# Low parts of normed operands, of the sums T1 to T4 and of the first gate and up weights on VectorE alone

## The chip, the cores and the metric

The kernel runs on one core of a Trainium2 chip. The core has a TensorE for matmuls (PE; its weight loads are PEld), VectorE (DVE), ScalarE (ACT), GpSimd (POOL) and a queue that issues DMAs (SP). The metric is the time on the device in microseconds, from one launch; each version is run several times and the median counts.

## The reference

The kernel computes two layers of an encoder for 1024 positions of width 1024, in float32. Cut to what matters here:

```
h = rms_norm(x, mix_norm_g[l])                 # x * rsqrt(mean(x*x) + eps) * g
proj = h @ w_in[l]                             # then three mixers: retention, RWKV-7, differential attention
x = x + mixed @ w_out[l]
h = rms_norm(x, ffn_norm_g[l])
hidden = silu(h @ w_gate[l]) * (h @ w_up[l])   # width 2816
x = x + hidden @ w_down[l]
...                                            # after both layers a last rms_norm
```

## The kernel before

All activations lie transposed: 8 row blocks of 128 features by two halves of 512 positions, so a tile is 128x512. The matmuls must be more exact than TensorE's fast format, so each operand is split: ScalarE copies it to the fast format (the high part, names ending in h: hh, sh, whh) and another engine subtracts the copy from the original (the low part: hl, sl, wll). `split` (lines 177 to 186) does both; its subtraction runs on VectorE unless `eng` says GpSimd. A product is then three matmuls, high by high, low by high and high by low (`dense`). In the names of the profile, h tiles are normed operands and T1, s tiles are T2 to T4, w tiles are weights; wr is a raw weight block from memory, ws a sum of weights.

The feed-forward part (`phase_c`) comes after the mixers. It first multiplies by w_out (`out_blocks`, PSUM tiles aps), norms both halves of the result (`norm_sq`, `norm_rs`, `norm_out`: squares on ScalarE, their sum on VectorE, a matmul with ones, nps, then logarithm and exponential on ScalarE, nrs, and a product on VectorE, line 262), and then computes gate and up in 11 pairs of column blocks (q = 0 to 10, 256 columns each). Each pair of each matrix is one Winograd-Strassen step over 2x2 blocks: seven block products instead of eight. The seven use the blocks B11, B21 and B22 of the normed input and its sums T1 to T4 (`ops_sums`: T1 = B12 - B11, T2 = B22 - T1, T3 = T2 - B11, T4 = B21 - T2, each for four row blocks), and of the weights A11, A12, A22 and four sums S1 to S4 (`set_first`, `set_rest`). The products are the tiles sp; there are seven PSUM banks for them. The input's low parts are made once per layer, at the start; the weights' low parts for each q. The wh and wl tiles have 8 buffers each, so a ninth weight part waits for the products that use the first.

Before the change, of the input's low parts GpSimd makes every second one of B11, B21, B22, T2 and T4 and all of T1 and T3, and it makes all of the weights'. The same alternation stands in `norm_split`, which norms the input of the mixers at each layer's start (tiles ntmp, products dps with w_in).

A scheduler sets the order of each engine's instructions from the program's order, its own estimates and priorities (`high_priority` around the norms). Each engine runs its queue strictly in order. During the mixers' input projection only one raw weight block fits (`wraw` is 1 with 4 row blocks), so the DMA of the next block is sent only when the high and the low part of the one before are made.

Of the kernel before, what the change touches and what calls it, by code (L numbers as in the profile page):

```python
# [177 lines left out]
class Net:  # L178
# [8 lines left out]
    def tt(self, out, a, b, op, eng=None):  # L187
        (eng or self.nc.vector).tensor_tensor(out=out, in0=a, in1=b, op=op)  # L188
# [87 lines left out]
    def norm_split(self, x, g, pool):  # L276

        h = [[], []]

        def emit(half, k, t):  # L280
            h[half].append(self.split(self.H, t, ("h", "h"), eng=self.nc.gpsimd if k % 2 else None))

        self.norm(x, g, pool, emit, (1, 0))
        return h
# [1004 lines left out]

    def op(self, ops, name, t, eng=None):
        p, tag = (self.S, "s") if name in ("T2", "T3", "T4") else (self.H, "h")
        ops[name].append(self.split(p, t, (tag, tag), eng=eng))

    def ops_sums(self, ops, bs, names=("T1", "T2", "T3", "T4")):

        g = self.nc.gpsimd
        for n in names:
            for i, (b11, b12, b21, b22) in enumerate(bs):  # L1300
                e = g if i % 2 else None
                if n == "T1":
                    self.tt(b12, b12, b11, ALU.subtract)
                    self.op(ops, n, b12, g)
                elif n == "T2":
                    self.tt(b22, b22, b12, ALU.subtract)
                    self.op(ops, n, b22, e)
                elif n == "T3":
                    self.tt(b11, b22, b11, ALU.subtract)
                    self.op(ops, n, b11, g)  # L1310
                else:
                    self.tt(b21, b21, b22, ALU.subtract)
                    self.op(ops, n, b21, e)

    def set_load(self, src):

        raw = []
        for a in src:
            r = self.W.tile([128, 8, 128], F32, tag="wr", name="wr", bufs=self.wraw)
            self.nc.sync.dma_start(out=r, in_=a)  # L1320
            raw.append(r)
        a, b = raw
        return dict(A11=a[:, :4], A12=a[:, 4:], A21=b[:, :4], A22=b[:, 4:], w={})

    def set_split(self, st, src, *names):

        hi, lo = self.split(self.W, src, ("wh", "wl"), eng=self.nc.gpsimd)
        n = src.shape[1] // len(names)
        for i, name in enumerate(names):
            st["w"][name] = [(hi[:, i * n + k], lo[:, i * n + k]) for k in range(n)]  # L1330
# [42 lines left out]

    def ffn_set(self, l, name, q):
        w = self.ia[name]
        return self.set_load([w[l, 2 * q], w[l, 2 * q + 1]])

    def ffn_first(self, st, ops):
        a = self.ft("as")
# [30 lines left out]
    def phase_c(self, l):  # L1410
        nc = self.nc
        acts = [[], []]
        for half in range(2):
            for k in range(8):
                m = self.S.tile([128, 512], F32, tag="s", name="mixl")
                nc.sync.dma_start(out=m, in_=self.mixed[k][:, half * 512:half * 512 + 512])
                acts[half].append(self.split(self.H, m, ("h", "h")))
        x = self.load_x(self.xs)
        self.out_blocks(l, x, acts)

        xm = [self.dr.tile([128, T], F32, name=f"xm{l}_{k}") for k in range(8)]
        ops = {n: [] for n in ("B11", "B21", "B22", "T1", "T2", "T3", "T4")}
        g = self.par[l][:, P_FFNG:P_FFNG + 8]
        n = [dict(pool=(self.S, "s")) for _ in range(2)]
        gp = nc.gpsimd
        with self.tc.high_priority(offset=100000):
            for half in range(2):
                for k in range(8):
                    nc.sync.dma_start(out=xm[k][:, half * 512:half * 512 + 512], in_=x[half][k])
            self.norm_sq(n[0], x[0], range(8))  # L1430
            self.norm_sq(n[1], x[1], range(4))
            self.norm_rs(n[0])
            for k in range(8):
                self.op(ops, "B21" if k >= 4 else "B11", self.norm_out(n[0], g, k, x[0], x[0][k]),
                        gp if k % 2 else None)
            self.norm_sq(n[1], x[1], range(4, 8))
            self.norm_rs(n[1])
            for k in (4, 5, 6, 7, 0, 1, 2, 3):
                t = self.norm_out(n[1], g, k, x[1], x[1][k])
                if k >= 4:  # L1440
                    self.op(ops, "B22", t, gp if k % 2 else None)
            self.ops_sums(ops, [(x[0][i], x[1][i], x[0][i + 4], x[1][i + 4]) for i in range(4)])

        hid = [self.dr.tile([128, T], F32, name=f"hid{l}_{f}") for f in range(NF)]
        for q in range(NF // 2):
            sets = []
            for name in ("w_gate", "w_up"):
                st = self.ffn_set(l, name, q)
                self.set_first(st)
                if q == 0:  # L1450
                    self.ffn_first(st, ops)
                    self.set_rest(st)
                    sets.append(st)
                else:
                    self.ffn_part(st, ops, sets, hid, q)
            if q == 0:
                done = []
                for st in sets:
                    self.ffn_part(st, ops, done, hid, q)
        return self.down(l, hid, xm)  # L1460
# [175 lines left out]
```

## Time and profile before

| | us |
|---|---|
| median of three runs | 3579.34 (3575.51 to 3581.64) |
| the profiled execution | 3579.7 |
| its span, first to last instruction | 3577.9 |
| TensorE busy | 3222.8 (90%) |
| VectorE busy | 2004.6 (56%) |
| ScalarE busy | 1576.7 (44%) |
| GpSimd busy | 943.7 (26%) |

The shares are means over stages with different limits. The stages that the change touches are short: layer 0's start (20 to 60 us of the span), layer 1's start (about 1784 to 1822) and the two feed-forward starts (about 1073 to 1160 and 2841 to 2930). What counts there is read from the order of the instructions in time and from what each waited for.

### The profile page before, as it was taken

The numbers are of one execution on the slowest core, as the hardware profiler recorded it, in microseconds if no ns is written. First come the engines' busy times: TensorE is split into PE (matmuls) and PEld (weight loads), VectorE is DVE, ScalarE is ACT, GpSimd is POOL, SyncE is SP. The second block draws the span as 40 slices with busy tenths as digits, with TensorE's granted clock in tenths as the row PEclk, the third lists the DMA queues.
The fourth block names the chain that finished last, engine by engine and source line by source line (L and its number), as shares of the span: only waits on it lengthen the run. The fifth ranks groups of instructions, "written<-read, shape, count | busy, mean of one in ns | idle before, by whom it ended". The sixth has DMA issues, their size and how long they took to land. (4 is left out here: it accounts for less than half of the span.)

```text
span 3577.9 us, 69843 instructions
## 1 busy us (share of the span) xinstructions
PE 3222.8 (90%) x28380; PEld 2601.8 (73%) x28380; DVE 2004.6 (56%) x3749; ACT 1576.7 (44%) x3071; POOL 943.7 (26%) x800
## 2 busy tenths in 40 slices
PE   6999797898787999999989997978986989999997
PEld 4777586787565888888867775867774758888886
DVE  4698425766329555552338974167662485555523
ACT  4566443666424333342236664346654342333322
POOL 3222120000026544532132221200000364554220
PEclk9999798998888999999989998989988989999998
DMA  5444334432341222283053433244325212223821
GB/s 167 154 147 123 112 106 132 145 124 72 127 146 47 86 80 83 83 285 121 26 161 123 151 117 118 96 143 139 122 83 175 83 59 80 86 83 99 278 71 47
DMA packets 214057, 418.93 MB, mean 117 GB/s; under 512 B 23876, under 2 KB 58948, under 8 KB 213700
## 3 DMA queue, kind: packets, MB, share of 16 engines
q1 hardware_dynamic: 191000, 378.53, 32.2%
q10 hardware_dynamic: 12672, 23.07, 1.7%
q0 software_dynamic: 10064, 12.85, 1.6%
q8 instruction: 224, 3.67, 0.4%
q14 instruction: 97, 0.79, 0.1%
HBM read 313.67 MB, written 100.70 MB: 116 GB/s over the span
## 5 line engine op out<-in xcount | busy, mean ns | idle before, releaser
L188 POOL TENSOR_TENSOR wll<-wr,whh 128x512 fp32r<-128x512 f32 x416 | 558.4, 1345 | 1616.8 <-ACT whh L185 1610.9
L185 ACT ACTIVATE whh<-wr 128x512 fp32r<-128x512 f32 x416 | 261.1, 631 | 625.8 <-PE sp L194 166.0
L194 PE MATMUL dps<-hl,whh 128*128 128x512 f32 x960 | 383.7, 400 | 6.6 <-DVE hl L188 3.6
L194 PE MATMUL dps<-hh,whh 128*128 128x512 f32 x960 | 387.7, 404 | 1.1 <-DVE stl L377 1.0
L194 PE MATMUL dps<-hh,wll 128*128 128x512 f32 x960 | 383.1, 399 | 0.4 <-POOL wll L188 0.4
L194 PE MATMUL sp<-hh,whh 128*128 128x512 f32 x704 | 279.2, 397 | 9.2 <-ACT hh L185 8.6
L194 PE MATMUL sp<-hl,whh 128*128 128x512 f32 x704 | 281.8, 400 | 2.1 <-POOL hl L188 1.9
L194 PE MATMUL sp<-hh,wll 128*128 128x512 f32 x704 | 276.9, 393 | 1.3 <-POOL wll L188 1.3
L194 PE MATMUL dn<-hl,whh 128*128 128x512 f32 x704 | 274.9, 391 | 0.5 <-DVE hl L188 0.5
L194 PE MATMUL dn<-hh,whh 128*128 128x512 f32 x704 | 274.1, 389 | 1.3 <-ACT hh L185 1.3
L194 PE MATMUL dn<-hh,wll 128*128 128x512 f32 x704 | 273.9, 389 | 0.0
L188 POOL TENSOR_TENSOR wll<-ws,whh 128x512 fp32r<-128x512 f32 x132 | 194.1, 1470 | 177.2 <-ACT whh L185 177.2
L188 DVE TENSOR_TENSOR hl<-hidr,hh 128x512 fp32r<-128x512 f32 x144 | 138.2, 977 | 170.4 <-ACT hh L185 161.5
L194 PEld LDWEIGHTS dps<-hl,whh 128*128 128x128 f32 x960 | 183.6, 191 | 51.8 <-POOL hl L188 6.1
L194 PE MATMUL sp<-sl,whh 128*128 128x512 f32 x528 | 211.3, 400 | 8.8 <-POOL sl L188 6.1
L194 PEld LDWEIGHTS dps<-hh,whh 128*128 128x128 f32 x960 | 183.7, 191 | 45.9 <-issue 4.4
L194 PE MATMUL sp<-sh,whh 128*128 128x512 f32 x528 | 209.8, 397 | 3.1 <-ACT as L185 3.1
L194 PEld LDWEIGHTS dps<-hh,wll 128*128 128x128 f32 x960 | 183.2, 191 | 38.8 <-issue 2.4
L194 PE MATMUL sp<-sh,wll 128*128 128x512 f32 x528 | 211.0, 400 | 0.0
L185 ACT ACTIVATE whh<-ws 128x512 fp32r<-128x512 f32 x132 | 83.5, 632 | 242.7 <-PE sp L194 138.5
L185 ACT ACTIVATE pt<-pt,mx 128x1024 f32<-128x1024 f32 x128 | 147.0, 1149 | 59.6 <-DVE mx L1216 57.3
L194 PEld LDWEIGHTS sp<-hh,whh 128*128 128x128 f32 x704 | 133.9, 190 | 41.1 <-ACT hh L185 9.4
(275 smaller groups left out, 7297.6 us busy)
## 6 DMA issues: line engine op xcount, KB each, us to landing
hidr<-hid SPq DMA_DIRECT2D x144, 256.0 KB, 4.9
bias<-t SPq DMA_DIRECT2D x64, 512.0 KB, 3.8
wr<-in_w_in_dram SPq DMA_DIRECT2D x120, 256.0 KB, 2.9
wr<-in_w_gate_dram SPq DMA_DIRECT2D x44, 512.0 KB, 3.4
wr<-in_w_up_dram SPq DMA_DIRECT2D x44, 512.0 KB, 3.3
wr<-in_w_down_dram SPq DMA_DIRECT2D x44, 512.0 KB, 4.1
pr<-st SPq DMA_DIRECT2D x56, 256.0 KB, 2.3
lo<-lod SPq DMA_DIRECT2D x48, 256.0 KB, 3.2
```

The source lines that it names most:

```text
L185: self.nc.scalar.activation(out=out, in_=in_, func=func, **kw)
L188: (eng or self.nc.vector).tensor_tensor(out=out, in0=a, in1=b, op=op)
L194: self.nc.tensor.matmul(out, lhsT, rhs, start=start, stop=stop, **kw)
```

## The change

`norm_split`, `op` and `ops_sums` no longer name GpSimd, so every low part of the normed operands and of T1 to T4 is made by VectorE. A set of weights carries its engine: for the first pair (q = 0) of gate and up it is VectorE, for the others GpSimd as before.

```diff
@@ norm_split
-            h[half].append(self.split(self.H, t, ("h", "h"), eng=self.nc.gpsimd if k % 2 else None))
+            h[half].append(self.split(self.H, t, ("h", "h")))
@@ op, ops_sums
-    def op(self, ops, name, t, eng=None):
+    def op(self, ops, name, t):
         p, tag = (self.S, "s") if name in ("T2", "T3", "T4") else (self.H, "h")
-        ops[name].append(self.split(p, t, (tag, tag), eng=eng))
+        ops[name].append(self.split(p, t, (tag, tag)))
...
-                    self.op(ops, n, b12, g)
+                    self.op(ops, n, b12)
...
@@ set_load, set_split, ffn_set
-    def set_load(self, src):
+    def set_load(self, src, eng):
...
-        return dict(A11=a[:, :4], A12=a[:, 4:], A21=b[:, :4], A22=b[:, 4:], w={})
+        return dict(A11=a[:, :4], A12=a[:, 4:], A21=b[:, :4], A22=b[:, 4:], w={}, eng=eng)
...
-        hi, lo = self.split(self.W, src, ("wh", "wl"), eng=self.nc.gpsimd)
+        hi, lo = self.split(self.W, src, ("wh", "wl"), eng=st["eng"])
...
-        return self.set_load([w[l, 2 * q], w[l, 2 * q + 1]])
+        return self.set_load([w[l, 2 * q], w[l, 2 * q + 1]], self.nc.gpsimd if q else None)
@@ phase_c
-                self.op(ops, "B21" if k >= 4 else "B11", self.norm_out(n[0], g, k, x[0], x[0][k]),
-                        gp if k % 2 else None)
+                self.op(ops, "B21" if k >= 4 else "B11", self.norm_out(n[0], g, k, x[0], x[0][k]))
...
-                    self.op(ops, "B22", t, gp if k % 2 else None)
+                    self.op(ops, "B22", t)
```

VectorE's queue in layer 0's feed-forward start, from the first of T3 on (x_11643, x_11645, x_11647 and x_11649 become T3, x_11651 and the next T4), before:

```order
L188 TENSOR_TENSOR x_11643<-x_11667,x_11643 128x512
L188 TENSOR_TENSOR sl_12347<-x_11671,sh_12346 128x512
L188 TENSOR_TENSOR x_11645<-x_11669,x_11645 128x512
L188 TENSOR_TENSOR x_11647<-x_11671,x_11647 128x512
L188 TENSOR_TENSOR x_11649<-x_11673,x_11649 128x512
L188 TENSOR_TENSOR x_11651<-x_11651,x_11667 128x512
L188 TENSOR_TENSOR x_11653<-x_11653,x_11669 128x512
L188 TENSOR_TENSOR x_11655<-x_11655,x_11671 128x512
```

And after, the same subtractions:

```order
L188 TENSOR_TENSOR x_11643<-x_11667,x_11643 128x512
L188 TENSOR_TENSOR sl_12352<-x_11673,sh_12351 128x512
L188 TENSOR_TENSOR x_11645<-x_11669,x_11645 128x512
L188 TENSOR_TENSOR sl_12357<-x_11643,sh_12356 128x512
L188 TENSOR_TENSOR x_11647<-x_11671,x_11647 128x512
L188 TENSOR_TENSOR sl_12362<-x_11645,sh_12361 128x512
L188 TENSOR_TENSOR x_11649<-x_11673,x_11649 128x512
L188 TENSOR_TENSOR sl_12367<-x_11647,sh_12366 128x512
L188 TENSOR_TENSOR x_11651<-x_11651,x_11667 128x512
L188 TENSOR_TENSOR sl_12372<-x_11649,sh_12371 128x512
```

Between the subtractions, where one low part of T2 stood, there is now one for each operand.

VectorE's queue behind the last sums there (c11 and c12 are sums of products, ws_12527 becomes S4 of the up weights, sl_12387 and sl_12392 are low parts of T4), before:

```order
L188 TENSOR_TENSOR sl_12377<-x_11651,sh_12376 128x512
L188 TENSOR_TENSOR x_11657<-x_11657,x_11673 128x512
L188 TENSOR_TENSOR c11_12444<-sp_12445,as_12429 128x512
L188 TENSOR_TENSOR sl_12387<-x_11655,sh_12386 128x512
L188 TENSOR_TENSOR c11_12512<-sp_12513,as_12497 128x512
L188 TENSOR_TENSOR ws_12527<-wr_12485,ws_12528 128x512
L188 TENSOR_TENSOR c12_12553<-sp_12554,as_12429 128x512
```

And after:

```order
L188 TENSOR_TENSOR sl_12387<-x_11655,sh_12386 128x512
L188 TENSOR_TENSOR c11_12444<-sp_12445,as_12429 128x512
L188 TENSOR_TENSOR sl_12392<-x_11657,sh_12391 128x512
L188 TENSOR_TENSOR c11_12512<-sp_12513,as_12497 128x512
L188 TENSOR_TENSOR wll_12532<-ws_12528,whh_12531 128x512
L188 TENSOR_TENSOR wll_12537<-wr_12487,whh_12536 128x512
L188 TENSOR_TENSOR wll_12541<-ws_12527,whh_12540 128x512
L188 TENSOR_TENSOR c12_12553<-sp_12554,as_12429 128x512
L188 TENSOR_TENSOR ws_12527<-wr_12485,ws_12528 128x512
```

S4 of the up weights (ws_12527 <- wr_12485, ws_12528) now stands behind three low parts of up weights and a further sum of products.

ScalarE's queue in layer 1's start (whh_17766 is the high part of the second weight block, whh_17836 of the third; nrs_17640 is the second half's norm factor, first the logarithm, then the exponential), before:

```order
L185 ACTIVATE nsq_17632<-x_17485 128x512
L185 ACTIVATE nsq_17635<-x_17500 128x512
L185 ACTIVATE whh_17766<-wr_17764 128x512
L185 ACT_TABLE_LOAD
L185 ACTIVATE nrs_17640<-nps_17638,eps_116 128x512
L185 ACT_TABLE_LOAD
L185 ACTIVATE nrs_17640<-nrs_17640 128x512
L185 ACTIVATE whh_17836<-wr_17834 128x512
L185 ACTIVATE hh_17645<-ntmp_17643 128x512
```

And after:

```order
L185 ACTIVATE nsq_17632<-x_17485 128x512
L185 ACTIVATE nsq_17635<-x_17500 128x512
L185 ACTIVATE whh_17766<-wr_17764 128x512
L185 ACTIVATE whh_17836<-wr_17834 128x512
L185 ACT_TABLE_LOAD
L185 ACTIVATE nrs_17640<-nps_17638,eps_116 128x512
L185 ACT_TABLE_LOAD
L185 ACTIVATE nrs_17640<-nrs_17640 128x512
L185 ACTIVATE hh_17645<-ntmp_17643 128x512
```

The third block's high part moved from behind the exponential to ahead of the first table load.

## Rows read from the trace of the kernel before

**Rows 1.** Busy time by stretch, layer 0: length, PE, PEld, DVE, ACT, POOL, PEclk, DMA.

```profile
1072.94:1098.33 25.39, 17.12 (x76) 13.86 (x74) 23.39 (x24) 11.69 (x20) 18.47 (x11) 0.92 0.21 72
1103.93:1141.34 37.41, 26.10 (x83) 16.64 (x83) 37.41 (x32) 15.19 (x25) 28.24 (x18) 0.86 0.00 0
...
1160.00:1180.00 20.00, 20.00 (x89) 16.25 (x88) 14.74 (x22) 7.53 (x13) 13.31 (x10) 1.00 0.39 135
```

**Rows 2.** TensorE in order of time, layer 0's feed-forward start: start, duration, [idle before <-releaser].

```profile
1098.39 2.08 PE L194 MATMUL nps<-nsq,ones 128*128 128x512 f32 x2 [8.33 <-DVE nsq L188]
...
1139.06 0.80 PE L194 MATMUL sp<-sh,whh 128*128 128x512 f32 x1 [1.56 <-ACT as L185]
...
1140.08 0.63 PE L194 MATMUL sp<-sh,wll 128*128 128x512 f32 x1
1140.51 0.63 PE L194 MATMUL sp<-sh,whh 128*128 128x512 f32 x1
...
1143.80 0.50 PE L194 MATMUL sp<-hh,whh 128*128 128x512 f32 x1 [0.33 <-ACT whh L185]
...
1145.42 0.50 PE L194 MATMUL sp<-hh,wll 128*128 128x512 f32 x1 [0.66 <-POOL wll L188]
```

**Rows 3.** The chain that ended last, layer 1's feed-forward start: start, length, piece.

```profile
2896.81 8.43 DVE x L188 x5
...
2913.39 86.83 PE sp L194 x375
```

**Rows 4.** VectorE in order of time, layer 0's feed-forward start.

```profile
1072.94 2.08 DVE L262 SCALAR_TENSOR_TENSOR x<-x,par,nrs 128x512 f32<-128x512 f32 x3 [3.22 <-ACT nrs L185]
...
1097.64 0.69 DVE L188 TENSOR_TENSOR nsq<-nsq 128x512 f32<-128x512 f32 x1 [0.70 <-ACT nsq L185]
1103.93 4.16 DVE L262 SCALAR_TENSOR_TENSOR x<-x,par,nrs 128x512 f32<-128x512 f32 x3 [5.59 <-ACT nrs L185]
...
1126.94 1.28 DVE L188 TENSOR_TENSOR x<-x 128x512 f32<-128x512 f32 x2
1128.14 0.68 DVE L188 TENSOR_TENSOR sl<-x,sh 128x512 fp32r<-128x512 f32 x1
1128.75 9.11 DVE L188 TENSOR_TENSOR x<-x 128x512 f32<-128x512 f32 x6
...
1140.66 0.68 DVE L188 TENSOR_TENSOR sl<-x,sh 128x512 fp32r<-128x512 f32 x1
```

**Rows 5.** GpSimd in order of time, the same stretch.

```profile
1071.03 1.29 POOL L188 TENSOR_TENSOR wll<-wr,whh 128x512 fp32r<-128x512 f32 x1 [25.96 <-ACT whh L185]
...
1128.37 8.34 POOL L188 TENSOR_TENSOR sl<-x,sh 128x512 fp32r<-128x512 f32 x5 [1.90 <-ACT sh L185]
```

**Rows 6.** VectorE in order of time, layer 0's start.

```profile
20.37 2.08 DVE L262 SCALAR_TENSOR_TENSOR ntmp<-x,par,nrs 128x512 f32<-128x512 f32 x3 [4.22 <-ACT nrs L185]
...
33.49 5.55 DVE L188 TENSOR_TENSOR nsq<-nsq 128x512 f32<-128x512 f32 x6
44.14 2.08 DVE L262 SCALAR_TENSOR_TENSOR ntmp<-x,par,nrs 128x512 f32<-128x512 f32 x3 [5.11 <-ACT nrs L185]
```

**Rows 7.** ScalarE in order of time, layer 0's start.

```profile
39.53 0.63 ACT L185 ACTIVATE whh<-wr 128x512 fp32r<-128x512 f32 x1 [4.46 <-DMA wr<-in_w_in_dram]
```

**Rows 8.** TensorE in order of time, layer 0's start.

```profile
58.38 0.50 PE L194 MATMUL dps<-hl,whh 128*128 128x512 f32 x1 [0.18 <-POOL hl L188]
```

**Rows 9.** ScalarE in order of time, layer 1's start.

```profile
1801.93 0.63 ACT L185 ACTIVATE whh<-wr 128x512 fp32r<-128x512 f32 x1 [3.55 <-DMA wr<-in_w_in_dram]
1802.59 1.28 ACT L185 ACT_TABLE_LOAD   x1
```

**Rows 10.** DMA issues of the page: count, KB each, us to landing.

```profile
wr<-in_w_in_dram SPq DMA_DIRECT2D x120, 256.0 KB, 2.9
```

**Rows 11.** VectorE in order of time, layer 1's start.

```profile
1807.56 3.12 DVE L262 SCALAR_TENSOR_TENSOR ntmp<-x,par,nrs 128x512 f32<-128x512 f32 x3 [4.83 <-ACT nrs L185]
```

**Rows 12.** GpSimd in order of time, layer 1's start.

```profile
1819.63 1.28 POOL L188 TENSOR_TENSOR hl<-ntmp,hh 128x512 fp32r<-128x512 f32 x1 [1.29 <-ACT hh L185]
```

More of the change, by code (lines that the diff above doesn't have):

```diff
@@ L1283, in diff_attend @@
             nc.sync.dma_start(out=self.mixed[6 + j][:, n4 * 512:n4 * 512 + 512], in_=t)
-    def op(self, ops, name, t, eng=None):
+    def op(self, ops, name, t):
         p, tag = (self.S, "s") if name in ("T2", "T3", "T4") else (self.H, "h")
-        ops[name].append(self.split(p, t, (tag, tag), eng=eng))
+        ops[name].append(self.split(p, t, (tag, tag)))
     def ops_sums(self, ops, bs, names=("T1", "T2", "T3", "T4")):
-        g = self.nc.gpsimd
         for n in names:
-            for i, (b11, b12, b21, b22) in enumerate(bs):
-                e = g if i % 2 else None
+            for b11, b12, b21, b22 in bs:
                 if n == "T1":
                     self.tt(b12, b12, b11, ALU.subtract)
-                    self.op(ops, n, b12, g)
+                    self.op(ops, n, b12)
                 elif n == "T2":
                     self.tt(b22, b22, b12, ALU.subtract)
-                    self.op(ops, n, b22, e)
+                    self.op(ops, n, b22)
                 elif n == "T3":
                     self.tt(b11, b22, b11, ALU.subtract)
-                    self.op(ops, n, b11, g)
+                    self.op(ops, n, b11)
                 else:
                     self.tt(b21, b21, b22, ALU.subtract)
-                    self.op(ops, n, b21, e)
-    def set_load(self, src):
+                    self.op(ops, n, b21)
+    def set_load(self, src, eng):
         raw = []
@@ L1424, in phase_c @@
         n = [dict(pool=(self.S, "s")) for _ in range(2)]
-        gp = nc.gpsimd
         with self.tc.high_priority(offset=100000):
```

## The prediction

> **What bounds the kernel now.** I first read the busy time by stretch [rows 1]. In the first microseconds behind the start (1160 to 1180 us) TensorE is busy for all 20.00 us at full clock: inside the feed-forward loop TensorE is the bound, and a microsecond won ahead of it stays won as long as that holds. At the start of the feed-forward part it is not so. From 1103.93 to 1141.34 VectorE is busy for 37.41 of 37.41 us and TensorE for 26.10, at 0.86 of the clock. The stretch before it, 1072.94 to 1098.33, shows 17.12 us of TensorE in 25.39. The second view is TensorE's own order in time [rows 2]: it waits 8.33 us for VectorE's sum of squares of the second half, and goes on without a gap only from 1145.42, behind a low part of a weight from GpSimd. Behind the wait that ends at 1139.06 the matmuls come 0.43 us apart (1140.08 and 1140.51); in the steady run of layer 1 there are 375 in 86.83 us, 0.23 each [rows 3]. So after such a wait TensorE runs at the lower of its two clocks, 1.2 and 2.4 GHz. The chain that ended last has the same stretch in layer 1 [rows 3]: VectorE's subtractions, and later 86.83 us of matmuls. So both layers pay this start once, with the same pattern.
>
> The third view is VectorE beside GpSimd [rows 4, 5]. GpSimd is idle for the 1.90 us before 1128.37. Two subtractions fall into that gap: they take 1.28 us and VectorE's next row starts 1.20 us after the first of them began, 0.60 each. When GpSimd then makes five low parts in a row, six subtractions of the same shape take 9.11 us, 1.52 each. GpSimd itself needs 1.67 for each of these five and 1.29 for one alone. So a low part on GpSimd costs VectorE about 0.9 us of slowdown, more than the 0.60 us that VectorE needs to make it.
>
> **The change, part by part.** Per feed-forward start 32 low parts leave GpSimd and come to VectorE: 14 of weights, 4 and 2 of the normed operands, 12 of the sums. GpSimd's next work is then the first low part of the second column pair's gate weights (q = 1), which stands behind all of this, so VectorE runs alone.
>
> *First half's norm to the sum of squares of the second.* In the new order VectorE has 8 norm products and 24 two-operand instructions from the first norm product to the last addition (8 low parts, 6 of weights, 4 additions of the output block, 4 of squares, 2 of weights' sums). With 0.69 for a product (2.08 for three [rows 4]) and 0.60 for the others that is 5.5 + 14.4 = 19.9 us, from 1072.94 to 1092.8. Before it ended at 1097.64 + 0.69 = 1098.33. The gain is 5.5 us. The output projection's last matmul does not stop it: TensorE had those done when its 8.33 us of waiting began, at 1090.06. The way from there to the next norm product stays at the 5.59 us of the row at 1103.93: the activation table load now stands behind two copies in ScalarE's queue, but all three fit beside VectorE's addition and the norm's matmul.
>
> *Second half's norm and the sums T1 to T4.* Before: 32 VectorE instructions from 1103.93 to 1140.66 + 0.68, 37.4 us. After: 8 products and 37 others (8 low parts of B22 and T1, 12 of T2 to T4, 16 subtractions, one sum of products), 5.5 + 22.2 = 27.7 us. The gain is 9.7 us. ScalarE's high part of each sum is covered: between a subtraction and its low part stand two other instructions (1.2 us) for a copy of 0.63 us [rows 9].
>
> *What is late next.* TensorE's next need is the high part of the up weights' S4, whose operand VectorE computes. Before, it came 1143.80 - 1141.34 = 2.5 us behind the last low part, and three matmuls of 0.23 us were done before the wait that ended at 1145.42, so the steady run begins in effect at 1144.7, 3.4 us behind. After, VectorE first has a sum of products, three low parts of up weights, another sum and then the operand: 6 x 0.60 = 3.6 us, then ScalarE's copy (0.63). TensorE, having waited for it, starts at the lower clock; some seven matmuls at 0.43 instead of 0.23, as after 1139.06, cost 1.4 us. That is 5.7 us against 3.4: a loss of 2.3.
>
> Sum for one start: 5.5 + 9.7 - 2.3 = 12.9 us; for the two layers 25.8. Bounds: with no clock loss and the up weights hidden 16; with VectorE at a whole 0.69 per instruction and 3 us more waiting behind the chain, 6.
>
> *Layer 0's start.* Here four more low parts of each half come to VectorE, which then makes all 8, while the weights' low parts stay on GpSimd and still collide. First half: 8 products (5.5), 8 low parts (4.8), the small instructions of lambda (0.7), one addition (0.6), and the six dependent additions, left at the row's 5.55 [rows 6]: 20.37 + 17.2 = 37.5 against 39.04. ScalarE's own way to the second norm goes through a weight block that a DMA brings at 39.53 [rows 7]; that DMA is sent when GpSimd's low part before it is done, so it comes earlier by about as much. I take 1.4 us. Second half: TensorE's last wait for a low part ended at 58.38 [rows 8]. After, that low part is the 14th instruction: 44.14 - 1.4 + 5.5 + 6 x 0.6 = 51.8, plus two collisions with GpSimd at 0.9 to 1.1, 54.0. The gain is 4.4 us (bounds 1.4 and 6.5); from 60 us on the matmuls run on.
>
> *Layer 1's start.* The same edit, but ScalarE's order turns against it: the high part of the third weight block now stands ahead of the table load and the logarithm of the second half. Its block can be sent only when GpSimd has the second block's low part. From the second's high part at 1801.93 [rows 9] that is 0.63 + 1.3 + 2.9 for the DMA [rows 10] = 1806.8; then 0.63, two table loads of 1.28 each, and logarithm and exponential at a copy's 0.63: the norm products begin at 1811.3, or at 1809.3 if the second block comes 2 us earlier, against 1807.56 [rows 11]. From there 8 products and 9 others take 10.9, and one collision 1: 1821.2 to 1823.2, where GpSimd's last low part ended at 1820.91 [rows 12]. The weights behind are ready earlier. I take a loss of 0.5 us (bounds: 1 gained, 3 lost).
>
> Together 25.8 + 4.4 - 0.5 = 29.7 us off the profiled 3579.7: 3550. The profiled execution lies 0.4 us above the median of the three, so nothing has to be shifted.
>
> On VectorE's 0.60 us: the low part of 0.68 at 1128.14 is followed by a start at 1128.75, 0.61 later [rows 4]. The Trainium skill (VectorE: DVE Perf Modes, The DRAIN you can't avoid) says that the next instruction does not start until the pipe of the one before is empty; by that each would cost its whole 0.68, and the trace does not agree.
>
> **The rivals.**
> 1. *TensorE waits in the first column pair behind VectorE's queue.* After the chain VectorE has 22 instructions (some 13.6 us) before it clears the first up product, and GpSimd's low parts for q = 1 run into them; four collisions of 1.1 us would reach TensorE through the product banks. Cost 4 to 5 us a layer: 3559. For it: VectorE had no idle time up to 1141.34 before [rows 1]. Against: five up products take TensorE 13.6 us too, so the queue just keeps up.
> 2. *Each VectorE instruction takes its whole duration.* 61 of them a layer lose 0.08 us: 4.9 a layer, 3560. The starts 0.60 apart speak against it. This is the skill's rule named above.
> 3. *Hidden anyway.* The loop behind the start is held by something other than TensorE, and only the layer starts pay: 3575. Against it stands the stretch after 1160 [rows 1].
> 4. *Slower: GpSimd is not what slows VectorE.* If VectorE's 1.52 us came from the ScalarE copies that read the same tiles, taking GpSimd away brings nothing, and 32 more instructions of 0.60 are 19.2 us against some 7.5 us of VectorE's idle time (5.59 and smaller ones): 12 us a layer, 3603. It decides once the collisions save less than 11.7 us per layer. Against it: ScalarE copies beside the two fast subtractions as well.
>
> **How the numbers follow.** Forecast 0.67, with its own range 3540 to 3556; rival 1 0.18, rival 2 0.05, rival 3 0.06, rival 4 0.04. No change is taken as within 0.2%, 7 us, about what can be told here. So faster 0.90, same 0.06, slower 0.04. The range, 3537 to 3566, takes both bounds of the starts: 2 x 16 + 6.5 + 1 = 39.5 off gives 3540 and a little more for what isn't seen; 2 x 6 + 1.4 - 3 = 10.4 off would be 3569, which I cut slightly.
>
> **What would show it.** In the changed profile GpSimd should be empty from about 1070 to 1125 us; VectorE's subtractions there should come 0.60 us apart, with low parts between them; the wait before the norm's matmul should shrink from 8.33 to about 2 us; the steady run of matmuls should begin near 1131 instead of 1145 in layer 0. In layer 1's first microseconds a ScalarE wait for a weight block should stand before the table load. Two fast subtractions beside a busy GpSimd, or slow ones without it, would make the forecast wrong.

## The result and the profile after

The changed kernel takes 3542.8 us (median of 4 runs, 3536.9 to 3546.0), the kernel before beside it 3577.4 (4 runs, 3574.6 to 3581.6): a ratio of 0.990, 95% interval 0.9883 to 0.9918, 34.6 us less. The forecast was 3550, 29.7 us less, with a range of 3537 to 3566. The profiled execution has a span of 3544.2 us, 33.7 less than before.

The times of the trace of after are its own: the layer-0 feed-forward start begins 6.45 us earlier in it than before (1066.49 against 1072.94). First the busy time by stretch, for the stretches of [rows 1]: the first half's first norm product to the end of the second half's sum of squares, the second half's first norm product to the last low part, and a piece of the steady run.

```profile
1066.49:1086.56 20.07, 17.81 (x79) 14.43 (x77) 20.00 (x33) 11.73 (x21) 0.00 (x0) 1.00 0.20 73
1091.30:1118.97 27.67, 21.07 (x77) 13.26 (x76) 27.67 (x46) 14.51 (x24) 0.00 (x0) 0.97 0.00 0
1140.00:1160.00 20.00, 20.00 (x88) 16.29 (x87) 13.49 (x18) 7.74 (x14) 13.67 (x10) 1.00 0.40 134
```

25.39 us have become 20.07, and 37.41 have become 27.67, though VectorE has 46 instructions in the second stretch where it had 32 (in each count the last one begins only some 0.1 us before the end). GpSimd is empty in both; its next row, from its own order in time, follows after 85.83 us of idleness:

```profile
1124.46 3.46 POOL L188 TENSOR_TENSOR wll<-wr,whh 128x512 fp32r<-128x512 f32 x2 [85.83 <-DVE wll L188]
```

VectorE in order of time, which answers to [rows 4]:

```profile
1066.49 2.08 DVE L262 SCALAR_TENSOR_TENSOR x<-x,par,nrs 128x512 f32<-128x512 f32 x3 [1.25 <-ACT nrs L185]
...
1091.30 2.08 DVE L262 SCALAR_TENSOR_TENSOR x<-x,par,nrs 128x512 f32<-128x512 f32 x3 [2.33 <-ACT nrs L185]
...
1105.02 0.70 DVE L188 TENSOR_TENSOR sl<-x,sh 128x512 fp32r<-128x512 f32 x1
1105.63 0.70 DVE L188 TENSOR_TENSOR x<-x 128x512 f32<-128x512 f32 x1
1106.23 0.70 DVE L188 TENSOR_TENSOR sl<-x,sh 128x512 fp32r<-128x512 f32 x1
...
1118.26 0.71 DVE L188 TENSOR_TENSOR sl<-x,sh 128x512 fp32r<-128x512 f32 x1
...
1121.86 0.71 DVE L188 TENSOR_TENSOR ws<-wr,ws 128x512 f32<-128x512 f32 x1
```

Subtractions and low parts follow each other 0.60 us apart, where six subtractions took 9.11 us before. TensorE there, for [rows 2]:

```profile
1086.62 1.98 PE L194 MATMUL nps<-nsq,ones 128*128 128x512 f32 x2 [2.31 <-DVE nsq L188]
...
1114.20 0.50 PE L194 MATMUL sp<-sl,whh 128*128 128x512 f32 x1 [0.23 <-DVE sl L188]
1114.54 0.40 PE L194 MATMUL sp<-sh,wll 128*128 128x512 f32 x1
1118.36 0.80 PE L194 MATMUL sp<-sh,whh 128*128 128x512 f32 x1 [3.43 <-ACT as L185]
1118.96 0.63 PE L194 MATMUL sp<-sl,whh 128*128 128x512 f32 x1
...
1123.65 0.63 PE L194 MATMUL sp<-hh,whh 128*128 128x512 f32 x1
1124.08 0.50 PE L194 MATMUL sp<-hl,whh 128*128 128x512 f32 x1
```

The wait before the norm's matmul has gone from 8.33 to 2.31 us. During the chain, VectorE's run from the second half's first norm product to the last low part of T4, TensorE waits 0.23 to 0.24 us at most of the low parts. Then it stands for 3.43 us, not for VectorE but for ScalarE's copy of the first up product (as), and does the twelve matmuls of T4's product behind it, 0.43 us apart, at a granted clock of 0.50 from 1118.36 to 1124.08. From there on there is no wait any more: TensorE is busy for all of the time to 1160. ScalarE in order of time shows both things that the forecast did not have:

```profile
1086.16 0.57 ACT L185 ACTIVATE as<-sp 128x512 f32<-128x512 f32 x1
1086.76 1.28 ACT L185 ACT_TABLE_LOAD   x1
1088.63 0.69 ACT L185 ACTIVATE nrs<-nps,eps 128x512 f32<-128x512 f32 x1 [0.60 <-PE nps L194]
1089.34 1.28 ACT L185 ACT_TABLE_LOAD   x1
1090.63 0.63 ACT L185 ACTIVATE nrs<-nrs 128x512 f32<-128x512 f32 x1
...
1117.73 0.58 ACT L185 ACTIVATE as<-sp 128x512 f32<-128x512 f32 x1
1122.66 0.63 ACT L185 ACTIVATE whh<-ws 128x512 fp32r<-128x512 f32 x1 [4.35 <-DVE ws L188]
```

The gate's copy as now stands ahead of the first table load and no longer between logarithm and exponential, and the up copy as stands behind the last high part of T4. Of the chain that ended last in layer 1 [rows 3], the pieces of GpSimd are gone. VectorE's remain but now last 0.60 to 0.70 us for most instructions, and behind them come only the last high part and the up copy as on ScalarE. So VectorE still sets the pace up to there, only faster. One piece of matmuls begins 27.1 us behind the second half's first norm product, where it began 41.5 us behind it before (2913.39 - 2871.90):

```profile
2847.26 2.08 DVE x L262 x3
...
2874.32 391.23 PE sp L194 x1685
```

At the layer starts, VectorE in layer 0 [rows 6]:

```profile
40.92 2.08 DVE L262 SCALAR_TENSOR_TENSOR ntmp<-x,par,nrs 128x512 f32<-128x512 f32 x3 [4.83 <-ACT nrs L185]
```

TensorE in layer 0, its last wait for a low part [rows 8]:

```profile
51.01 0.51 PE L194 MATMUL dps<-hl,whh 128*128 128x512 f32 x1 [0.30 <-DVE hl L188]
```

ScalarE in layer 1 [rows 9], which does wait 4.15 us for the third weight block ahead of the table load:

```profile
1783.24 0.63 ACT L185 ACTIVATE whh<-wr 128x512 fp32r<-128x512 f32 x1 [4.15 <-DMA wr<-in_w_in_dram]
1783.89 1.28 ACT L185 ACT_TABLE_LOAD   x1
```

And VectorE in layer 1 [rows 11]:

```profile
1787.85 2.08 DVE L262 SCALAR_TENSOR_TENSOR ntmp<-x,par,nrs 128x512 f32<-128x512 f32 x3 [6.08 <-ACT nrs L185]
```

To place the gain, the trace was cut at the first norm product of each norm:

| stretch, us | before | after |
|---|---|---|
| layer 0: first half's to second half's norm products | 23.8 | 22.0 |
| layer 0: from there through the mixers to the feed-forward start | 1028.8 | 1025.6 |
| feed-forward 0: first half's to second half's norm products | 31.0 | 24.8 |
| feed-forward 0: from there to the next layer's first norm product | 679.9 | 671.6 |
| layer 1: first half's to second half's norm products | 23.7 | 24.9 |
| layer 1: from there to the feed-forward start | 1033.3 | 1035.2 |
| feed-forward 1: both stretches | 31.0 + 680.2 | 24.2 + 670.6 |

The two feed-forward parts give 14.5 and 16.4 us. The rest is 2.8 us, of which 1.4 lies ahead of the first norm product. That 1.4 is not the change's: in ffn_only and weights_only below, whose layer starts are as before, the first norm product also comes 1.0 and 1.3 us earlier than in the profile before (19.35 and 19.07 against 20.37).

### The profile page after: what moved, and what is told of

Its sections match the earlier page's. It is cut to its first block, busy times and chain, and to the rows that moved or that the text cites. A ratio compares the mean times of both kernels' runs of the same rounds, so it can differ in the third digit from the quotient of the medians.

```text
span 3544.2 us, 69804 instructions
## 1 busy us (share of the span) xinstructions
PE 3215.1 (91%) x28380; PEld 2598.1 (73%) x28380; DVE 1983.1 (56%) x3829; ACT 1573.0 (44%) x3071; POOL 814.7 (23%) x720
## 5 line engine op out<-in xcount | busy, mean ns | idle before, releaser
L188 POOL TENSOR_TENSOR wll<-wr,whh 128x512 fp32r<-128x512 f32 x400 | 534.0, 1338 | 1805.7 <-ACT whh L185 1625.6
L188 POOL TENSOR_TENSOR wll<-ws,whh 128x512 fp32r<-128x512 f32 x120 | 175.5, 1462 | 176.4 <-ACT whh L185 170.3
L194 PEld LDWEIGHTS sp<-hl,whh 128*128 128x128 f32 x704 | 133.0, 189 | 34.3 <-DVE hl L188 5.5
```

Of the source, the lines that this page charges most:

```text
L194: self.nc.tensor.matmul(out, lhsT, rhs, start=start, stop=stop, **kw)
```

## The experiments

Theory: a low part on GpSimd costs VectorE more than VectorE needs to make it, and VectorE paces TensorE at the feed-forward starts. The main rival is the fourth: something else slows VectorE. "Stretch" below is the time from a feed-forward part's first norm product to the next norm's first, of layer 0 and layer 1; "first part" is the time to the second half's first norm product, of layer 0. Medians of 4 to 12 runs; after_again to rest_early ran on one chip beside 13 runs of the kernel before (3577.4), sums_only to s4_in_chain beside 17 (3578.5), the last two beside 9 (3580.5).

| run | median | ratio to before, 95% interval | first part | stretch 0, 1 |
|---|---|---|---|---|
| before (profile) | 3577.4 | 1 | 31.0 | 710.9, 711.2 |
| changed (profile) | 3542.8 | 0.9883 to 0.9918 | 24.8 | 696.4, 694.8 |
| after_again | 3545.4 | 0.9897 to 0.9925 | 24.2 | 696.0, 695.7 |
| ffn_only | 3547.4 | 0.9898 to 0.9930 | 24.8 | 696.3, 696.9 |
| dup | 3589.8 | 1.0020 to 1.0049 | 29.0 | 716.1, 716.0 |
| rest_early | 3550.1 | 0.9908 to 0.9938 | 26.1 | 698.2, 696.8 |
| sums_only | 3565.8 | 0.9947 to 0.9971 | 30.4 | 705.0, 705.7 |
| weights_only | 3573.0 | 0.9977 to 0.9995 | 28.5 | 706.5, 706.9 |
| s4_first | 3540.0 | 0.9878 to 0.9904 | 24.6 | 694.1, 694.1 |
| s4_in_chain | 3546.8 | 0.9903 to 0.9927 | 24.2 | 695.9, 695.1 |
| after_pair | 3543.9 | 0.9877 to 0.9910 | 24.2 | 695.6, 695.3 |
| s4_first_pair | 3540.1 | 0.9870 to 0.9898 | 24.6 | 694.3, 692.9 |

**The reference (after_again).** No edit.

> The changed kernel once more, beside the others on one chip: some 34 us faster than the kernel before, as first measured. It is the reference for the three runs beside it.

32 us faster here. Five of the six first parts of the changed kernel measure 24.2 us, one 24.8; in the shorter ones the norm's two matmuls run at the higher clock (granted 1.00 there in this run, 0.53 in the longer one):

```profile
1089.70 1.13 PE L194 MATMUL nps<-nsq,ones 128*128 128x512 f32 x2 [2.35 <-DVE nsq L188]
```

**Without the edit at the layer starts (ffn_only).**

```diff
@@ norm_split
-            h[half].append(self.split(self.H, t, ("h", "h")))
+            h[half].append(self.split(self.H, t, ("h", "h"), eng=self.nc.gpsimd if k % 2 else None))
```

> The change without its edit at the layer starts: norm_split alternates between VectorE and GpSimd as before, the feed-forward starts stay as changed. Theory (the gain is made at the two feed-forward starts, by the traces 14.4 and 15.7 us, and the layer starts bring 3 to 4 us in all): 30 us faster than before, 3547, and 3 to 5 us slower than the full change. By the terms of the prediction (25.8 at the feed-forward starts, 3.9 at the layer starts) 25.8 us faster, 3551. Rival (the 5 us won at layer 0's start and the 3 us won at layer 1's start are taken back inside the mixers, which wait for other things): as fast as the full change within 1 us.

2.0 us slower than the full change, with intervals that overlap. So the feed-forward starts bring nearly all: 30 us of 32. The layer starts are too small to be told here. From a layer's first norm product to its feed-forward start, nine profiles with the edit (all runs but ffn_only and weights_only) take 1046.9 to 1054.0 us in layer 0 and 1052.0 to 1060.1 in layer 1, though most of them have the same instructions there; the three without it 1050.5 to 1052.6 and 1054.6 to 1057.1. The means differ by 2.4 us for the edit in layer 0 and 1.0 against it in layer 1, well inside that scatter. That neither expectation of 3 to 5 us nor that of nothing is excluded is the honest reading.

**GpSimd's low parts once more, for nothing (dup).** VectorE makes every low part as in the changed kernel, and GpSimd makes 18 per layer again, into the same tiles.

```diff
@@ op
-        ops[name].append(self.split(p, t, (tag, tag)))
+        hi, lo = self.split(p, t, (tag, tag))
+        if name in ("T1", "T3") or len(ops[name]) % 2:
+            self.split_lo(lo, t, hi, self.nc.gpsimd)
+        ops[name].append((hi, lo))
```

> The full change, and in the feed-forward starts GpSimd makes again the 18 low parts per layer of B11, B21, B22 and T1 to T4 that it made before, into the same tiles behind VectorE, so that VectorE's own work is as in the changed kernel and GpSimd's nearly as in the kernel before. Theory (a GpSimd low part that runs beside VectorE costs VectorE 0.9 us): 14 of them in the second half's chain lengthen it from 27.7 by 12.6 to 40.3 us, 4 more the first part by 3.6, so 16 us a layer: 3543 + 32 = 3575, about the kernel before; VectorE's instructions there 1.5 to 1.7 us whenever GpSimd is busy. Rival 4 (GpSimd is not what slows VectorE, ScalarE's copies are): the chain stays at 27.7 us, TensorE gets the last low parts of T3 and T4 1 to 2 us later, 3545 to 3549.

44 us slower than the changed kernel beside it, and slower than the kernel before. Busy time by stretch, as above, of this run:

```profile
1068.36:1092.50 24.14, 17.80 (x79) 14.42 (x77) 24.07 (x33) 11.76 (x21) 6.87 (x4) 0.95 0.17 61
1097.31:1138.87 41.56, 27.91 (x81) 17.48 (x80) 41.56 (x46) 14.50 (x24) 21.85 (x13) 0.74 0.00 1
```

The same 33 and 46 VectorE instructions take 24.14 and 41.56 us instead of 20.07 and 27.67: 4.1 us for 4 low parts of GpSimd and 13.9 for 13, so 1.0 to 1.1 each. VectorE in order of time shows which instructions pay:

```profile
1122.71 0.68 DVE L188 TENSOR_TENSOR x<-x 128x512 f32<-128x512 f32 x1
1123.32 1.76 DVE L188 TENSOR_TENSOR sl<-x,sh 128x512 fp32r<-128x512 f32 x1
1125.00 0.68 DVE L188 TENSOR_TENSOR x<-x 128x512 f32<-128x512 f32 x1
1125.60 1.75 DVE L188 TENSOR_TENSOR sl<-x,sh 128x512 fp32r<-128x512 f32 x1
```

And GpSimd beside it:

```profile
1122.87 1.66 POOL L188 TENSOR_TENSOR sl<-x,sh 128x512 fp32r<-128x512 f32 x1 [1.83 <-DVE sl L188]
1125.16 1.65 POOL L188 TENSOR_TENSOR sl<-x,sh 128x512 fp32r<-128x512 f32 x1 [0.63 <-DVE sl L188]
```

The instruction that runs while GpSimd has a low part takes 1.75 us, its neighbours 0.68; ScalarE's copies are the same in both kernels (24 in the stretch). With that the fourth rival falls. The total was 3575 by the expectation and came to 3590: the chain was right (41.56 against 40.3), but TensorE now also waits for GpSimd's second writing, 0.2 to 2.4 us at a time, and ran at a granted clock of 0.74 in this stretch against 0.97.

**The sums alone (sums_only) and the weights alone (weights_only).** In the first the q = 0 weights stay on GpSimd; in the second they alone move.

```diff
@@ ffn_set, on the changed kernel (sums_only)
-        return self.set_load([w[l, 2 * q], w[l, 2 * q + 1]], self.nc.gpsimd if q else None)
+        return self.set_load([w[l, 2 * q], w[l, 2 * q + 1]], self.nc.gpsimd)
@@ set_load, set_split, ffn_set, on the kernel before (weights_only)
...
+        return self.set_load([w[l, 2 * q], w[l, 2 * q + 1]], self.nc.gpsimd if q else None)
```

> The change without its edit on weights: the low parts of the first gate and up weights (14 per layer) stay on GpSimd, all others go to VectorE. Theory (a low part on GpSimd costs VectorE 0.9 to 1.0 us while it runs, on VectorE 0.60): 6 of them fall into the first part (6 x 0.37 = 2.2 us longer than in the changed kernel), about 4 into the chain of the second half, which holds no weights in the changed kernel (4 x 0.97 = 3.9): 6 us a layer lost, 3543 + 12 = 3555. From the first norm product of one feed-forward start to the next norm's first: 702 us, where the changed kernel has 696 and the kernel before 711. Rival (only the operands' low parts matter, since TensorE waits for them): 3543 to 3546.

> Only the edit on weights: the 14 low parts of the first gate and up weights go to VectorE, the operands' low parts stay divided as in the kernel before. Theory: the first part 1.5 us longer than in the changed kernel (4 low parts on GpSimd at 0.97 instead of 0.60 on VectorE), the chain 5.2 us longer (14 of them), so of the 15 us that the change brings a layer 8 remain: 3577 - 16 = 3561, 703 us from norm product to norm product. Rival (only the operands' low parts matter): 3574 to 3578.

Both missed by 11 to 12 us, on the slow side. The gains per stretch are 5.7 and 4.4 us, together 10.1, where the two edits in one bring 15.4. Of the misses, 6.7 and 7.4 us lie in the two stretches (705.4 and 706.7 us where 702 and 703 were expected); where the rest comes from stays open. The expectations had reckoned a low part on GpSimd at 0.97 us, less 0.60 where VectorE saves one, and no more. Busy time of the first part and of the chain in sums_only:

```profile
1071.41:1096.25 24.84, 17.12 (x76) 13.85 (x74) 24.05 (x28) 11.84 (x20) 11.24 (x7) 0.93 0.23 83
1101.85:1133.70 31.85, 22.56 (x78) 14.61 (x77) 31.85 (x46) 15.10 (x25) 6.36 (x4) 0.89 0.00 0
```

In the chain 4 low parts cost 4.2 us, as expected. In the first part VectorE has 28 instructions and not 33, 3.0 us fewer, and is yet busy for 24.05 us and not 20.00: 7.05 us for 7 low parts, 1.0 each, of which the expectation counted 6 at 0.37. And the way to the second half's norm products stays at 5.60 us, since ScalarE's as copy falls between logarithm and exponential again. In weights_only the cost lies elsewhere. VectorE in order of time:

```profile
1108.28 4.29 DVE L188 TENSOR_TENSOR x<-x 128x512 f32<-128x512 f32 x7
...
1119.72 0.68 DVE L188 TENSOR_TENSOR c<-sp,as 128x512 f32<-128x512 f32 x1
```

GpSimd there:

```profile
1109.70 11.22 POOL L188 TENSOR_TENSOR hl<-x,hh 128x512 fp32r<-128x512 f32 x1 [3.22 <-ACT hh L185]
```

And TensorE:

```profile
1120.97 0.80 PE L194 MATMUL sp<-hl,whh 128*128 128x512 f32 x1 [10.80 <-POOL hl L188]
```

Here VectorE's subtractions go at 0.60 us beside GpSimd, and one low part of GpSimd takes 11.22 us instead of 1.29, in layer 1 too. TensorE waits 10.80 us for it, and GpSimd then makes the other low parts, 1.53 us each, with TensorE behind it. So mixed work loses on one engine or on the other, and what the sums and the weights bring apart is less than what an empty GpSimd brings.

**What is late next (rest_early, s4_first, s4_in_chain).** Three orders of the same instructions behind the chain: all sums and splits of the first weights at high priority; only S1 and S4 of the up weights first, with both c11 additions early; the same with S1 and S4 ahead of T1.

```diff
@@ phase_c (rest_early; ScalarE's as copy as below)
+                    with self.tc.high_priority(offset=100000):
                         self.set_rest(st)
@@ ffn_first (s4_first, s4_in_chain)
+        with self.tc.high_priority(offset=200000):
+            self.act(a, p)
...
+        with self.tc.high_priority(offset=200000):
+            self.tt(c11, p, a, ALU.add)
@@ set_rest for w_up at q = 0 (s4_first: offset 0; s4_in_chain: 100000)
+            with self.tc.high_priority(offset=0):
+                self.set_split(st, s1, "S1")
+                self.tt(s1, st["A12"], s2, ALU.subtract)
+                self.set_split(st, s1, "S4")
+            self.set_split(st, s2, "S2")
...
```

> The full change, with the sums and splits of the first gate and up weights (set_rest) put under high priority, so that S4 of the up weights and its low part, and ScalarE's copy of the first up product, come before the end of the chain T1 to T4 and not behind it; TensorE's S4 product lies between the T4 matmuls. In the changed kernel TensorE stands 3.43 us before T4's first matmul, then does T4 and S4 after the chain's end at the lower clock. Theory (what is late next is the wait for that copy and S4): some 8 VectorE instructions of 0.60 move ahead, 4.8 us, but 24 matmuls of 0.43 no longer follow the chain; 2 to 4 us gained a layer, 3535 to 3539. Rival 1 (VectorE's queue is the bound up to the first hidden block, in whatever order): within 2 us of the changed kernel.

> The full change, with three moves and no instruction added: the additions c11 of gate and up and ScalarE's copy of the first up product stand ahead of the chain's end, so that a PSUM bank is free when T4's first matmul could start; and of the up weights S1 and S4 are split first, S2 and S3 behind them. Theory (late next after the chain is not VectorE as a whole but this bank, and then S4): T4's matmuls keep pace with VectorE, the chain ends 1.2 us later, S4's product starts 1.5 us behind the chain's end instead of 4.7: 1 to 3 us gained a layer, 693 to 695 us from norm product to norm product where the changed kernel has 696, in all 3538 to 3542. Rival (VectorE's queue holds the end in any order, as the run with all of the sums moved ahead may mean): 696 to 697 us, 3543 to 3546.

> As the run beside it, but S1 and S4 of the up weights are made early in the chain (three VectorE instructions, 1.8 us, ahead of T1) and TensorE's S4 product lies between T4's matmuls. Theory: the chain ends 3 us later than in the changed kernel, but 24 matmuls then end with it, 693 to 695 us from norm product to norm product; rival (waits for weight buffers in ScalarE's queue hold the chain, as they did when all of the sums were moved ahead: 1.0 to 1.7 us each): 697 us or more.

rest_early gained nothing (stretches 1 to 2 us longer): its first part is 26.1 us, since instructions were put ahead of the second half's norm, and in the chain VectorE waits for ScalarE, which waits for a weight buffer. ScalarE in order of time:

```profile
1110.34 0.63 ACT L185 ACTIVATE whh<-wr 128x512 fp32r<-128x512 f32 x1 [1.48 <-PE sp L194]
```

And VectorE:

```profile
1111.00 0.69 DVE L188 TENSOR_TENSOR wll<-wr,whh 128x512 fp32r<-128x512 f32 x1 [1.00 <-ACT whh L185]
```

The order let in something else, too: GpSimd makes two low parts of the next pair's weights inside the chain, where the changed kernel has none. It is the same in s4_in_chain. VectorE there:

```profile
1117.30 1.71 DVE L188 TENSOR_TENSOR sl<-x,sh 128x512 fp32r<-128x512 f32 x1
```

And GpSimd:

```profile
1116.88 1.58 POOL L188 TENSOR_TENSOR wll<-wr,whh 128x512 fp32r<-128x512 f32 x1 [75.37 <-ACT whh L185]
```

VectorE's other low parts beside these last 0.68 us, so each of the two costs about 1.0 us, as in dup. s4_in_chain is as fast as the changed kernel; the 693 to 695 us that its theory gave did not come (695.9 and 695.1). s4_first did what its theory said. TensorE in order of time:

```profile
1118.56 0.50 PE L194 MATMUL sp<-sl,whh 128*128 128x512 f32 x1 [0.24 <-DVE sl L188]
...
1119.76 0.50 PE L194 MATMUL sp<-sl,whh 128*128 128x512 f32 x1 [0.23 <-DVE sl L188]
1120.10 0.39 PE L194 MATMUL sp<-sh,wll 128*128 128x512 f32 x1
1121.03 0.50 PE L194 MATMUL sp<-hh,whh 128*128 128x512 f32 x1 [0.54 <-ACT whh L185]
1121.36 0.39 PE L194 MATMUL sp<-hl,whh 128*128 128x512 f32 x1
```

The wait for the as copy is gone, T4's matmuls keep pace with VectorE, and S4's product begins 30.2 us behind the second half's first norm product (1121.03 - 1090.84), not 32.4 (1123.65 - 1091.30). The stretches are 694.1 in both layers. The last two runs repeated it beside the changed kernel:

> The changed kernel on the same chip as the run with S4 first, as its reference: 3543 to 3546; 695 to 697 us from norm product to norm product in both layers.

> S4 of the up weights first and the two c11 additions early, once more beside the changed kernel. By the trace of its first run (694.1 us from norm product to norm product in both layers, where three runs of the changed kernel have 694.8 to 696.4) it is 2 to 5 us faster than the changed kernel beside it. If the 1.8 us a layer were chance, the medians lie within 2 us and the stretches at 695 to 696.

3540.1 against 3543.9, and stretches of 694.3 and 692.9 against 695.6 and 695.3. All four stretches of s4_first are shorter than all eight of the changed kernel and of ffn_only (694.8 to 696.9); by the medians alone, whose intervals overlap, 3.8 us could not be told. It is the fastest version here.

## Why the prediction was right, point by point

1. *First half's norm to the sum of squares of the second: right.* 19.9 us forecast, 20.07 measured, a gain of 5.3.
2. *The way from there to the norm product: wrong, by 0.9 us.* It was taken to stay at 5.59 and is 4.74 (1091.30 - 1086.56). The forecast counted what stands ahead of the table load and not what leaves the place behind the logarithm: the as copy of 0.60 us and a wait of 0.16 stood there before. Where TensorE stays at the higher clock, another 0.6 us go (1.13 for the norm's matmuls instead of 1.98).
3. *The chain: right to the tenth.* 27.7 forecast, 27.67 measured; the 0.60 us per instruction held throughout. With that the second rival falls. The sentence of the Trainium skill that the prediction sets beside it (VectorE: DVE Perf Modes, The DRAIN you can't avoid) is not the whole of that section, which goes on that a next instruction starts earlier where it is not held back. The trace agrees with that: 0.60 us between starts, 0.70 for each instruction.
4. *What is late next: right in kind, wrong in its mechanism, and over-priced.* 2.3 us were taken as lost, for a wait on S4's high part and seven matmuls at the lower clock. Measured, with the stretch behind the second half's first norm product at 671.3 us (mean of six) against 680.0 (two, of one profile), 8.7 of the 9.7 us remain: 1.0 was lost. S4's high part came at 1123.29 (1122.66 + 0.63) and found TensorE still at T4's product, because that had waited for a PSUM bank that ScalarE's as copy held. The lower clock did cost: twelve matmuls 0.43 us apart behind the chain, at a granted clock of 0.50, where s4_first has 1.00 from its chain's start at 1090.84 to 1130. s4_first shows that bank and S4's place together are worth 1.8 us a layer.
5. *Sum per feed-forward start:* 12.9 forecast, 15.4 measured (711.05 less 695.6, the mean of six), just inside the bound of 16. Twice that is 31 of the 34.6 us. This is the mis-sized term: points 2 and 4, 2.5 us a layer, 5 of the 5 to 7 us by which the forecast was too slow.
6. *Layer 0's start: right at its own place.* The first half's norm gained 1.8 us (1.4 forecast) and TensorE's last wait for a low part came at 51.01 - 18.93 = 32.1 us behind the first norm product instead of 38.0, 5.9 us earlier (4.4 forecast, bounds 1.4 and 6.5). What of it passes through the mixers stays open.
7. *Layer 1's start: the forecast reordering happened, with a smaller price.* The norm products begin 1.2 us later than before, 24.9 against 23.7 us behind the first ones (1.7 to 3.7 forecast): the way from the second weight block's high part to the third's took 4.78 us (4.83 forecast), but the second came 2.6 us earlier (1778.46 - 1762.93 against 1801.93 - 1783.82), where the forecast allowed 2. The last low part was then done 36.2 us behind the first norm product (1797.35 + 1.80 - 1762.93), before 37.1, and the loss of 0.5 us could not be told from nothing.
8. *The rivals.* The first (TensorE behind VectorE's queue in the first column pair) did not come: no wait behind 1124.08. The third (hidden anyway) falls by the stretches, the fourth by dup. What the prediction named as a sign against itself, fast subtractions beside a busy GpSimd, did not come in the changed kernel, where GpSimd is empty, but it came in weights_only: the price of about 1 us holds for streams in which GpSimd gets in, as in the kernel before, dup and sums_only, and not for every pair of instructions that meet.

On the cause, the Trainium skill (SBUF — State Buffer, Who interferes with whom) says that a VectorE instruction with two inputs from SBUF contends with a GpSimd instruction that reads SBUF. The runs agree: 1.75 us instead of 0.68 for the VectorE instruction, 1.65 instead of 1.29 for GpSimd's, and 1.0 us on VectorE's queue for each low part.

## What to carry to other kernels

Price a second engine's help by what it does to the first: read one instruction with and without company from the trace, and where a helper's instruction costs the bound engine more (1.0 us here) than doing the work itself (0.60), take all of it away, since half a move can bring less than half (4.4 and 5.7 us a layer here against 15.4 together). When a stall goes, look in the queues of all engines for what stood between its two ends and for who holds the banks; that is where both errors of size lay. Moving late work forward helps only as far as it doesn't lengthen the chain that it is moved past, and it can let the helper's next work into that chain (two low parts in s4_in_chain).

## What the runs showed of the hardware that was not expected

Beside each other, either engine can be the one that is held back. Before, GpSimd came in at every turn and VectorE's subtractions took 1.52 us [rows 4, 5]. In weights_only a GpSimd low part that began at 1109.70, 0.22 us behind the start of a VectorE subtraction, lasted 11.22 us, while 16 VectorE instructions began 0.60 us apart; it ended 1.20 us behind the start of c<-sp,as, the first VectorE instruction there with an input in PSUM. The section of the Trainium skill on who interferes with whom, named above, says that a VectorE instruction with at most one input from SBUF, outside the modes that use both ports, does not contend with GpSimd, which fits this end. It also says that the order of issue decides who blocks. But in the kernel before GpSimd's four low parts of T1 begin at the same distance from a VectorE subtraction and get in. VectorE there:

```profile
1117.90 2.35 DVE L188 TENSOR_TENSOR x<-x 128x512 f32<-128x512 f32 x2
```

And GpSimd:

```profile
1118.12 6.66 POOL L188 TENSOR_TENSOR hl<-x,hh 128x512 fp32r<-128x512 f32 x4 [1.89 <-ACT hh L185]
```

1118.12 is 0.22 us behind 1117.90, yet the next subtraction takes 1.7 us and the low parts 1.67 each. What decides it was not found.

Additions that depend on each other come further apart than the 0.60 us of independent ones. Three additions of the sum of squares ahead of layer 0's feed-forward start in the changed kernel, with GpSimd idle:

```profile
1060.98 2.29 DVE L188 TENSOR_TENSOR nsq<-nsq 128x512 f32<-128x512 f32 x3 [0.35 <-ACT nsq L185]
```

One lasts 0.69 us, so they begin 0.80 us apart. The seven in layer 1's start take 6.93 us together, but two of them met a low part of GpSimd there (1.20 and 1.72 us long).
